# The gate product as seven block products, with its operands made during the MLP and kept in DRAM

## The chip, the core and the metric

The kernel runs on one core of one Trainium2 chip. The metric is device time in microseconds (us): the median over executions of the whole program. The core has a matrix engine (PE, with its weight loads shown apart as PEld), a vector engine (DVE), a scalar engine (ACT), a general engine (POOL), and a queue engine (SP) that issues nearly all of the DMAs. Each engine executes its own list of instructions in order; semaphores tie the lists together. Data lives in SBUF (128 partitions), PE writes to eight PSUM banks, and tensors too large for SBUF go to DRAM.

## The reference

One transformer layer over 1024 + 256 = 1280 tokens of width 1024: attention of two kinds, an output projection, a squared-ReLU MLP of inner width 4096, then the stage that the change rewrites, and a final norm. Its last part is

```python
n2 = _rms_norm(h, g_mlp, NORM_EPS)
a = jax.nn.relu(jnp.einsum('bsd,df->bsf', n2, w_ff1))
h = h + jnp.einsum('bsf,fd->bsd', a * a, w_ff2)

gate = jax.nn.sigmoid(jnp.einsum('bsd,de->bse', _rms_norm(h, g_ple, NORM_EPS), w_ple_gate))
h = h + gate * jnp.einsum('bsp,pd->bsd', p_l, w_ple_proj)
return h                      # then _rms_norm(h, g_final, NORM_EPS)
```

The gate product is 1280 x 1024 by 1024 x 1024; the embedding product is 1280 x 256 by 256 x 1024.

## The kernel before

Every matrix product is made of three: each fp32 operand is split into a high part (rounded to the format that PE reads fast, an ACT copy) and a low part (the rest, a subtraction on DVE or POOL), and high x high, high x low and low x high are summed in one PSUM bank. In the code this is `split3` (L156) or a list of pairs such as (a, b).

The MLP already uses a scheme of seven block products in place of eight (Strassen's, in Winograd's form). Tokens, inner width and columns are each halved; with HP = 5 token tiles of 128 in a half. Its second product, h += (a*a) w_ff2, is the loop over m = 0 to 55: seven block products in the order `O2 = (1, 7, 6, 4, 5, 3, 2)`, of eight steps m each. `put2(m)` is one step on PE: for each of the five tiles six matmuls of 512 columns, into five banks that are held over the eight steps. `prep(m)` makes the operands of step m: ACT writes the high parts of `ao` (128x1280) and `wo` (128x1024), and DVE the low parts. For products 7 and 5 DVE also subtracts two raw weight pieces (`w2r`, 128x1024), and for 7 and 6 POOL updates the kept piece `kt` (128x1024) for the next block product. `prep(m + 3)` is written behind `put2(m)`, since `ao` and `wo` have three slots each; so an operand set is made while PE is two steps ahead of its use. `load2(m)` fetches from DRAM two steps earlier still. After the last step of a block product, `evac2` adds the five banks into the quarters of h: product 6, the third, has the most of it, with fifteen adds on DVE and ten on POOL.

The gate stage takes the ten token tiles one after the other, FORD, each with both column halves: `gate_input` transposes the tile on PE (eight transposes), splits it, and computes the row scale; `gate(i)` runs 24 matmuls of 512 columns per half (the last tile's second half in two pieces of 256 columns), then the sigmoid: exp on ACT, a `tensor_scalar` on DVE, ln and exp on ACT, a multiplication on POOL (`gd`), and a `scalar_tensor_tensor` on DVE. `embed` is six matmuls per half; `add` multiplies (DVE, from PSUM), subtracts into h (POOL; DVE for the last two tiles) and sums squares (ACT). The final norm scales each half on DVE and stores it. The weights of the gate product (g_ple times w_gate, split) and of the embedding are made in SBUF towards the end of the MLP.

The order on each engine comes from a scheduler that simulates the program once at build time; the kernel's own code order is where it starts from. What it places is fixed at run time, and each engine waits at the head of its list.

Of the kernel before, what the change touches and what calls it, by code (L numbers as in the profile page):

```python
# [23 lines left out]
P = 128  # L24
# [21 lines left out]
def encoder_kernel(ctx: ExitStack, tc: tile.TileContext, x, xT, pT, w_in, w_out, w_ff1, w_ff2, w_gate, w_proj,  # L46
# [161 lines left out]
    def open_slots(pool_, tags):  # L208
        for tag in tags:
            slot_pool[tag] = pool_  # L210
            size = {"H": 2560, "L": 2560, "W": 1024, "Q": 1280, "K": 1280, "T": 512}[tag[0]]
            slot(tag, [P, size], F32, tag)
# [1128 lines left out]
    open_slots(fq, ["Q2", "Q3"])  # L1341
# [8 lines left out]
    AOS, WOS, ARS, WRS = ("H0", "H2", "H3"), ("H1", "L7", "L5"), ("L1", "L6"), ("W8", "W9", "Q0", "Q1", "Q2", "Q3")  # L1350
# [3 lines left out]
    kt2 = {}  # L1354
    wr_n = itertools.count()
    w2v = w_ff2.rearrange("(b c x r) n -> b x r c n", c=2, x=2, r=P)

    def load2(m):
# [3 lines left out]
        t = AR[m] = slot(ARS[m % 2], [P, 2, HT], F32, "ar")  # L1362
        dma(t, ad[i][b].rearrange("c p t -> p c t"))
        WR[m] = []
        for x, y in WSRC[i]:
            if i == 1:
                t = kt2[b] = slot(KTS[b], [P, 2, 512], F32, "kt2")
            else:
                t = slot(WRS[next(wr_n) % 6], [P, 2, 512], F32, "w2r")
                WR[m].append(t[:])  # L1370
            dma(t, w2v[b, x][:, :, y * 512:y * 512 + 512])
# [29 lines left out]
    def load_h(half, n, tag):  # L1401
# [4 lines left out]
    BANKS = ("f2 pj f1 f2 tr", "pj tr f1 f2 pj", "f2 tr f1 pj tr", "f2 pj f1 f2 tr", "tr pj f1 f2 pj",  # L1406
             "f1 f2 tr tr pj", "f1 f2 pj f1 f2")
# [68 lines left out]
    FORD = [TORD[2 * j + h] for h in (1, 0) for j in range(HP)]  # L1476
    gw, pw, n3 = [], [], {}
    g_n = itertools.count()

    def w_raw(src):  # L1480
        n = next(g_n)
        t = slot("W10" if n < 4 else f"W{8 + n % 2}", [P, D], F32, "graw")
        dma(t, src)
        return t

    def gate_w(k, tags):
        raw = w_raw(w_gate[k * P:(k + 1) * P, :])
        if len(tags) == 1:
            t = at32(tags[0], [P, 2, D], F32R, "gw")
            a, b = t[:, 0], t[:, 1]  # L1490
        else:
            a, b = (slot(t, [P, D], F32R, "gw")[:] for t in tags)
        S.activation(a, raw, AF.Copy, scale=gple[:, k:k + 1])
        V.scalar_tensor_tensor(b, raw, gple[:, k:k + 1], f(a), op0=ALU.mult, op1=ALU.subtract)
        gw.append((a, b))

    def proj_w(k, tag):
        raw = w_raw(w_proj[k * P:(k + 1) * P, :])
        t = at32(tag, [P, 2, D], F32R, "pw")
        S.activation(t[:, 0], raw, AF.Copy)  # L1500
        V.tensor_tensor(t[:, 1], raw, f(t[:, 0]), op=ALU.subtract)
        pw.append((t[:, 0], t[:, 1]))

    gi_n = itertools.count()

    def h_half(t, n):
        j, half = divmod(TORD.index(t), 2)
        return h_of(j, half, n)

    def gate_input(t):  # L1510

        n3_ = at32(("H5", "L4")[next(gi_n) % 2], [P, 2, KD, P], F32R, "n3")
        n3h, n3l = n3_[:, 0], n3_[:, 1]
        for n in range(2):
            tr = pp2[0].tile([P, 4, P], F32, tag="tr", name="trg", bufs=2)
            for k in range(4):
                PE.transpose(tr[:, k], h_half(t, n)[:, k * P:(k + 1) * P], ident)
            S.activation(n3h[:, 4 * n:4 * n + 4], tr, AF.Copy)
            V.tensor_tensor(n3l[:, 4 * n:4 * n + 4], tr, f(n3h[:, 4 * n:4 * n + 4]), op=ALU.subtract)
        ss = gq_.tile([P, 2], F32, tag="gss", name="gss")  # L1520
        for n in range(2):
            jk = gq_.tile([P, 512], F32, tag="gjk", name="gjk", bufs=1)
# [174 lines left out]
```

## Time and profile before

| what | value |
|---|---|
| time, median of 3 runs | 1690.53 us (1689.94 to 1693.5) |
| the profiled execution's own time | 1691.84 us |
| its span in the trace | 1690.1 us |
| PE busy over the span | 1651.6 us (98%) |
| DVE, ACT, POOL busy | 1179.9, 868.0, 661.0 us |
| second product of the MLP | about 1152 to 1535 us |
| gate stage | about 1535 us to the end |
| last matmul's end | about 1679 us |

Times in the trace are counted from the span's start. A row of the timeline gives the start, the duration, the engine, the line, the operation, output<-inputs, how many, and in brackets how long the engine was idle before and what ended that. A row of groups ends in busy time and the mean duration in ns. The view of one line gives min/median/max in ns. The table by windows gives each engine's busy time in a stretch, the granted PE clock (1.00 is full), the share of the DMA engines that was busy, and GB/s. PE's busy time is modelled, so it is read together with the distances between matmuls.

### The profile page before, as it was taken

Reading aid. Unit: us, or ns where it says so; the run is one execution under the profiler, and the core shown is the slowest. Engines: PE = TensorE matmul, PEld = TensorE weight load, DVE = VectorE, ACT = ScalarE, POOL = GpSimd, SP = SyncE. Lnnn points to the kernel's source line nnn. Section 1 sums busy time; section 2 is a strip of 40 time slices with the busy share of each in tenths; the row PEclk is TensorE's granted clock in tenths of the full one; section 3 lists DMA queues with packets and bytes.
Section 4 is the critical chain, followed back from the end, with each engine's and each line's share of the span. In section 5 each row is a group of like instructions: output and inputs, shape, how many; then the busy total and the mean of one; then the engine's idle time right before and its main releaser. Section 6 shows DMA issues by size and latency. Waiting matters only on the chain.

```text
span 1690.1 us, 27269 instructions
## 1 busy us (share of the span) xinstructions
PE 1651.6 (98%) x9849; PEld 1482.7 (88%) x9849; DVE 1179.9 (70%) x2119; ACT 868.0 (51%) x1749; POOL 661.0 (39%) x647
## 2 busy tenths in 40 slices
PE   8999999999899999999999999999999999999997
PEld 8999888888788888889999999998888888888886
DVE  7778588777888888668666666666665855445666
ACT  8643377776766667674333333233433333354554
POOL 1223455555654445433566665620532400001441
PEclk9999999999999999999999999999999999999999
DMA  9766843433954524395443343349676356532111
GB/s 309 239 216 237 247 144 110 133 108 98 273 161 130 154 74 131 108 330 172 160 136 131 132 159 128 135 169 386 220 225 203 124 192 210 177 117 75 35 44 50
DMA packets 191867, 278.28 MB, mean 165 GB/s; under 512 B 13674, under 2 KB 121076, under 8 KB 191732
## 3 DMA queue, kind: packets, MB, share of 16 engines
q1 hardware_dynamic: 189988, 271.28, 49.7%
q0 software_dynamic: 1600, 5.24, 1.0%
q8 instruction: 78, 1.28, 0.3%
q14 instruction: 57, 0.47, 0.1%
q10 hardware_dynamic: 144, 0.00, 0.0%
HBM read 182.63 MB, written 88.61 MB: 160 GB/s over the span
## 4 chain that ended last, share of the span: by engine, by line
PE 79%; DVE 8%; ACT 4%; issue 4%; POOL 2%; DMA 2%; POOLq 0%; SPq 0%; ACTq 0%; DVEq 0%
PE psa L264 6%; PE sc L651 6%; PE av L729 5%; PE psb L264 4%; PE pso L264 4%; PE tr L705 4%; PE psv L264 2%; PE psg L1588 1%; DVE pl L716 1%; DVE p L686 1%; DMA xt<-in_x 1%; POOL hq L1615 1%; DMA xr<-in_xT 1%; PE f__15605 L156 1%; PE f__16642 L156 1%
## 5 line engine op out<-in xcount | busy, mean ns | idle before, releaser
L1384 ACT ACTIVATE ao<-ar 128x1280 fp32r<-128x1280 f32 x56 | 71.2, 1273 | 183.7 <-PE f__15946 L156 36.6
L651 PE MATMUL sc<-kt,qt 128*128 128x512 f32 (+1 forms) x576 | 156.6, 392 | 8.8 <-ACT p L676 6.1
L716 DVE TENSOR_TENSOR pl<-tr,ph 128x512 fp32r<-128x512 f32 x204 | 138.0, 685 | 32.0 <-ACT ph L711 30.8
L1386 DVE TENSOR_TENSOR ao<-ar,ao 128x1280 fp32r<-128x1280 f32 x56 | 93.3, 1666 | 85.2 <-ACT ao L1384 85.2
L711 ACT ACTIVATE ph<-tr 128x512 fp32r<-128x512 f32 x204 | 120.0, 596 | 59.2 <-PE tr L705 52.7
L651 PEld LDWEIGHTS sc<-kt,qt 128*128 128x128 f32 x576 | 98.8, 189 | 27.1 <-ACT p L676 7.6
L264 PE MATMUL pso<-ow,mt 128*128 128x512 f32 x480 | 119.9, 396 | 2.0 <-DVE osq L756 1.3
L705 PE MATMUL tr<-ident,p 128*128 128x128 f32 x768 | 116.0, 274 | 5.8 <-DVE pl L716 5.1
L1588 PE MATMUL psg<-gw,n 128*128 128x512 f32 (+1 forms) x504 | 113.7, 381 | 0.0
L705 PEld LDWEIGHTS tr<-ident,p 128*128 128x128 f32 x768 | 91.6, 141 | 22.6 <-DVE pl L716 9.0
L1105 POOL TENSOR_SCALAR w1r<-w1r,gmlp 128x256 f32<-128x256 f32 x112 | 80.3, 735 | 68.4 <-DMA w1r<-in_w_ff 68.4
L1588 PEld LDWEIGHTS psg<-gw,n 128*128 128x128 f32 x504 | 90.9, 188 | 17.8
L264 PEld LDWEIGHTS pso<-ow,mt 128*128 128x128 f32 x480 | 88.0, 189 | 19.9 <-DVE osq L756 2.0
L729 PE MATMUL av<-ph,vt 128*128 128x256 f32 x544 | 101.8, 288 | 1.0 <-ACT ph L711 0.4
L690 POOL TENSOR_SCALAR p<-p,rl 128x1024 f32<-128x1024 f32 x64 | 76.2, 1192 | 50.6 <-DVE rl L688 49.1
L1178 ACT ACTIVATE w<-w1s 128x512 fp32r<-128x512 f32 x56 | 35.2, 629 | 114.7 <-POOL w1s L1185 55.3
L668 DVE TENSOR_REDUCE mm<-sc 128x1 f32<-128x1024 f32 (+1 forms) x80 | 84.2, 1056 | 9.4 <-PE sc L651 9.0
L729 PE MATMUL av<-pl,vt 128*128 128x256 f32 x408 | 89.4, 300 | 0.0
L729 PEld LDWEIGHTS av<-ph,vt 128*128 128x128 f32 x544 | 81.8, 188 | 6.4 <-DVE osq L756 0.8
L676 ACT ACTIVATE p<-sc,mm 128x1024 f32<-128x1024 f32 x64 | 71.4, 1116 | 25.1 <-DVE mm L668 16.3
L664 DVE CUSTOM_DVE_ANT_0 p<-sc,dist 128x1024 f32<-128x1024 f32 x64 | 77.6, 1218 | 7.8 <-PE sc L651 3.8
L673 ACT ACTIVATE p<-p,mm 128x1024 f32<-128x1024 f32 x64 | 73.5, 1149 | 18.0 <-DVE mm L664 17.2
(1520 smaller groups left out, 4705.9 us busy)
## 6 DMA issues: line engine op xcount, KB each, us to landing
ar<-ad SPq DMA_DIRECT2D x56, 640.0 KB, 4.0
w2r<-in_w_ff SPq DMA_DIRECT2D x56, 512.0 KB, 4.6
qt<-qd SPq DMA_DIRECT2D x160, 128.0 KB, 3.0
ad<-q SPq DMA_DIRECT2D x64, 320.0 KB, 2.8
ad<-qs SPq DMA_DIRECT2D x48, 320.0 KB, 2.2
w1r<-in_w_ff SPq DMA_DIRECT2D x28, 512.0 KB, 4.3
md<-ml SPq DMA_DIRECT2D x40, 256.0 KB, 2.5
mt<-md SPq DMA_DIRECT2D x20, 512.0 KB, 5.7
```

Of the source, the lines that this page charges most:

```text
L264: PE.matmul(ps, a, b, start=i == 0, stop=i == n - 1)
L651: PE.matmul(ps[:, h0:h0 + n], shared["q"][:, cc, v, i * P:(i + 1) * P], kt[:, s0 + h0:s0 + h0 + n], start=v == 0, stop=v == 1)
L664: V.tensor_tensor_reduce(out=p[:, :sn], in0=ps[:, :sn], in1=dst_t[:, off:off + sn], scale=SLOPES[idx], scalar=3.0e38, op0=ALU.add, op1=ALU ...
L668: V.tensor_reduce(out=st["m", i][:, 0:1], in_=ps[:, :sn], axis=AX.X, op=ALU.max, negate=True)
L690: G.tensor_scalar(p[:, :sn], p[:, :sn], rl[:, 0:1], 1.0, op0=ALU.mult, op1=ALU.mult)
L705: PE.transpose(t[:, jj, i * P:(i + 1) * P], st["ws"][i][:, j * P:(j + 1) * P], ident)
L711: S.activation(ph, st["tr", j2], AF.Copy)
L716: V.tensor_tensor(pl, st["tr", j2], f(st["ph", j2][:]), op=ALU.subtract)
L729: PE.matmul(st["av"][:, :256], x_, y_, start=j2 == 0 and n == 0, stop=j2 == nj - 1 and n == len(pr) - 1)
L1105: G.tensor_scalar(raw[:, k], raw[:, k], gmlp[:, 4 * kh + k:4 * kh + k + 1], 1.0, op0=ALU.mult, op1=ALU.mult)
L1386: V.tensor_tensor(ao[:, 1], a, f(ao[:, 0]), op=ALU.subtract)
L1588: ends[:] = [PE.matmul(ps, a, b, start=m == 0, stop=m == len(pr) - 1)]
```

## The change

The gate product is cut as the MLP's products are: tokens in two halves of five tiles, inner width and columns in halves of 512, and seven block products in place of eight, in the order `ORDER = (1, 2, 6, 5, 3, 7, 4)`. A block product is five tiles of twelve matmuls (four inner pieces of 128, times three). Products 1, 6 and 5 only feed sums (`m1`, `u3`); after each tile of products 2, 3, 7 and 4 one quarter of the gate is complete: `gate_half` adds the sum to the bank (DVE, from PSUM), takes the sigmoid, and combines. The tile's final norm follows after product 3 (second token half) and product 4 (first). After product 7 POOL multiplies the tile's h by `gfin` ahead, and for these halves ACT does the last scaling.

Operands of the token side are transposed quarters of h (`RA`): three of the four quarters are transposed during the last three block products of the MLP, the fourth in the gate stage; POOL and DVE form the sums and differences (four operations on 128x512 per tile), and `a_op` splits them. Operands of the weight side are made by `gate_operands`, a generator that the MLP's loop advances once per step from m = 4 on: for each half x of the pieces it loads four raw pieces, scales them by g_ple (POOL, 8 x 128x512), forms differences (POOL, 4 x 128x1024), and splits each of seven operands in two pieces (`out`: ACT copy, DVE subtraction, store of 512 KB to `bed`). The embedding's weights (4 x 512 KB) and embeddings (10 x 256 KB) go the same way to `pwd` and `ped`. The gate stage loads them back (`b_ops`, `proj_w`, `embed_in`). PSUM banks "tr" are freed of the MLP's fifth and sixth block product; slots in SBUF are shared out anew.

```diff
@@ the MLP's loop
     for m in range(NM):
         put2(m)
         if m in QUADS:
             load_h(*QUADS[m])
         if m + 3 < NM:
             prep(m + 3)
-        if m >= 4 * NB and m % 4 == 0 and len(gw) < 4:
-            gate_w(len(gw), KTS[2 * len(gw):2 * len(gw) + 2])
...
+        n, b = divmod(m, NB)
+        if m >= 4:
+            with tc.issue_after(fetched[0].ins):
+                next(made, None)
+        if n == 4 and b < HP:
+            if b == 0:
+                raw_tokens("H5", 12)
+            S.activation(RA[12][:, b], quad_tr(12, b), AF.Copy)
...
@@ gate_operands
+        def out(y, src, dst):
+            S.activation(stage[:, y, 0], src, AF.Copy)
+            V.tensor_tensor(stage[:, y, 1], src, f(stage[:, y, 0]), op=ALU.subtract)
+            dma(dst, f(stage[:, y]))
+
+        for x in range(2):
...
+            for t, k0, c0 in ((r11, 4, 0), (r22, 0, 512), (r12, 4, 512), (r21, 0, 0)):
+                k0 += 2 * x
+                dma(t, w_gate[k0 * P:(k0 + 2) * P, c0:c0 + 512].rearrange("(k p) c -> p k c", p=P))
+                for y in range(2):
+                    G.tensor_scalar(t[:, y], t[:, y], gple[:, k0 + y:k0 + y + 1], 1.0, op0=ALU.mult, op1=ALU.mult)
+            yield
+            for i, t, a, b, op in ((1, r11, None, None, None), (3, r22, None, None, None), (2, r21, None, None, None),
+                                   (7, r22, r22, r12, ALU.subtract), (5, r12, r12, r11, ALU.subtract),
+                                   (6, r11, r11, r22, ALU.add), (4, r21, r21, r11, ALU.subtract)):
+                if op is not None:
+                    G.tensor_tensor(t, a, b, op=op)
+                for y in range(2):
+                    out(y, t[:, y], bed[i][2 * x + y])
+                yield
@@ gate stage
-            for k in range(KD):
-                pr += [(n3h[:, k], gw[k][0][:, n]), (n3h[:, k], gw[k][1][:, n]), (n3l[:, k], gw[k][0][:, n])]
...
+    def product(i, j, c0=0, cn=512):
+        ps = bank(next(gslots), "psg")[:, :cn]
+        pr = []
+        for k in range(4):
+            a, w = AOPS[i][j], BOPS[i][k]
+            c = slice(c0, c0 + cn)
+            pr += [(a[:, 0, k], w[:, 0, c]), (a[:, 0, k], w[:, 1, c]), (a[:, 1, k], w[:, 0, c])]
...
+        ps, _ = product(i, j)
+        e = e_tile()
+        V.tensor_tensor(e, ps, acc_, op=ALU.add)
+        if i == 7:
+            V.tensor_tensor(m1[:, j], ps, m1[:, j], op=ALU.add)
+        sigmoid(e, e, rn, late)
+        combine(half, j, 512 * n, 512, e, embed(p, 512 * n, 512), n, late)
+        if i in (3, 4):
+            finish(half, j)
+        elif i == 7:
+            h = h_of(j, half, 1)
+            G.tensor_tensor(h, h, gfin[:, 1], op=ALU.mult)
```

What this does to the order of instructions is seen at three places. In all of them `ao`, `wo`, `w2r` and `kt` belong to the MLP's second product, as above.

The first is DVE's list around the MLP's second to third block product (products 7 and 6), before:

```order
L1379 TENSOR_TENSOR w2r<-w2r 128x1024
L1387 TENSOR_TENSOR wo<-w2r,wo 128x1024
L1386 TENSOR_TENSOR ao<-ar,ao 128x1280
L1387 TENSOR_TENSOR wo<-w2r,wo 128x1024
L1386 TENSOR_TENSOR ao<-ar,ao 128x1280
L1387 TENSOR_TENSOR wo<-w2r,wo 128x1024
L1386 TENSOR_TENSOR ao<-ar,ao 128x1280
L1387 TENSOR_TENSOR wo<-kt_14319,wo 128x1024
```

and in the change (`gbs` is the stage from which the gate's weight operands are stored, `gr` the raw pieces):

```order
L1384 TENSOR_TENSOR w2r<-w2r 128x1024
L1392 TENSOR_TENSOR wo<-w2r,wo 128x1024
L1391 TENSOR_TENSOR ao<-ar,ao 128x1280 x2
L1534 TENSOR_TENSOR gbs<-gr,gbs 128x512
L1392 TENSOR_TENSOR wo<-w2r,wo 128x1024
L1534 TENSOR_TENSOR gbs<-gr,gbs 128x512
L1391 TENSOR_TENSOR ao<-ar,ao 128x1280
L1392 TENSOR_TENSOR wo<-kt_14320,wo 128x1024
L1391 TENSOR_TENSOR ao<-ar,ao 128x1280
L1534 TENSOR_TENSOR gbs<-gr,gbs 128x512 x2
```

The subtractions of the gate's weights stand between those of the MLP's operands, which PE waits for; in DVE's list there are 23 of them from just ahead of the first `wo` of product 7 to just behind the first `wo` of product 4.

The second is POOL's list in the same stretch. Before, it holds only the updates of `kt` and the adds into h:

```order
L1390 TENSOR_TENSOR kt_14497<-w2r,kt_14497 128x1024
L1428 TENSOR_TENSOR hq<-hq,acc 128x512 x5
L1390 TENSOR_TENSOR kt_14548<-w2r,kt_14548 128x1024
L1390 TENSOR_TENSOR kt_14594<-w2r,kt_14594 128x1024
L1390 TENSOR_TENSOR kt_14634<-w2r,kt_14634 128x1024
L1390 TENSOR_TENSOR kt_14676<-w2r,kt_14676 128x1024
```

In the change:

```order
L1545 TENSOR_SCALAR gr<-gr,gple 128x512 x8
L1395 TENSOR_TENSOR kt_14389<-w2r,kt_14389 128x1024
L1433 TENSOR_TENSOR hq<-hq,acc 128x512 x3
L1551 TENSOR_TENSOR gr<-gr 128x1024
L1433 TENSOR_TENSOR hq<-hq,acc 128x512 x2
L1395 TENSOR_TENSOR kt_14495<-w2r,kt_14495 128x1024
L1551 TENSOR_TENSOR gr<-gr 128x1024
L1395 TENSOR_TENSOR kt_14545<-w2r,kt_14545 128x1024
L1551 TENSOR_TENSOR gr<-gr 128x1024
L1395 TENSOR_TENSOR kt_14635<-w2r,kt_14635 128x1024
L1551 TENSOR_TENSOR gr<-gr 128x1024
```

Scalings and differences of the gate's weights (`gr`) stand among the updates of `kt`; a second set of both follows in product 6.

The third is POOL's list in the gate stage. Before, one tile half takes two operations, and a tile a third (`p_l`):

```order
L1569 TENSOR_TENSOR p_l<-pr,p_h 128x256
L1596 TENSOR_TENSOR gd<-gd,ge 128x512
L1615 TENSOR_TENSOR hq<-hq,ge 128x512
L1596 TENSOR_TENSOR gd<-gd,ge 128x512
L1615 TENSOR_TENSOR hq<-hq,ge 128x512
```

In the change, around product 7 of the gate (L1756 is the multiplication ahead by `gfin`; a tile that lies in the `gfin` slot carries its name):

```order
L1658 TENSOR_TENSOR gd<-gd,ge 128x512
L1756 TENSOR_TENSOR hq<-hq,gfin 128x512 x2
L1666 TENSOR_TENSOR hq<-hq,ge 128x512
L1658 TENSOR_TENSOR gd<-gd,gfin 128x512
L1658 TENSOR_TENSOR gd<-gd,ge 128x512
L1756 TENSOR_TENSOR hq<-hq,gfin 128x512
L1666 TENSOR_TENSOR hq<-hq,gfin 128x512
```

A tile half there takes three operations. On PE the list has 432 matmuls of the gate product where it had 504 (24 of them of 256 columns, before 48), and 80 transposes of h in both.

More of the change, by code (lines that the diff above doesn't have):

```diff
@@ new lines, in encoder_kernel, with e_tile @@
+    e_n = itertools.count()
+    gfin = None
+    def e_tile():
+        if gfin is not None:
+            n = next(e_n) % 7
+            if n % 2:
+                return gfin[:, 2 + n // 2]
+        return gq_.tile([P, 512], F32, tag="ge", name="ge", bufs=4)[:]
+    def product(i, j, c0=0, cn=512):
+        ps = bank(next(gslots), "psg")[:, :cn]
+        pr = []
+        for k in range(4):
+            a, w = AOPS[i][j], BOPS[i][k]
+            c = slice(c0, c0 + cn)
+            pr += [(a[:, 0, k], w[:, 0, c]), (a[:, 0, k], w[:, 1, c]), (a[:, 1, k], w[:, 0, c])]
+        ends = []
+        for n, (a, w) in enumerate(pr):
+            ends[:] = [PE.matmul(ps, a, w, start=n == 0, stop=n == len(pr) - 1)]
+        return ps, ends[0]
```

379 lines of the change are left out of this document (235 added, 144 removed).

## The prediction

> **What bounds the kernel now.** I read the busy times first, then the table by windows, since an average over stages says little.
>
> ```profile
> PE 1651.6 (98%) x9849; PEld 1482.7 (88%) x9849; DVE 1179.9 (70%) x2119; ACT 868.0 (51%) x1749; POOL 661.0 (39%) x647
> ...
> 1200.00:1250.00 50.00, 50.00 (x222) 41.42 (x221) 37.95 (x20) 20.47 (x21) 25.29 (x10) 1.00 0.71 228
> ...
> 1625.00:1650.00 25.00, 25.00 (x116) 20.75 (x115) 14.48 (x25) 13.70 (x38) 10.85 (x9) 1.00 0.08 27
> ...
> 1675.00:1691.00 16.00, 4.08 (x29) 3.62 (x27) 9.53 (x25) 6.68 (x19) 0.00 (x0) 0.74 0.18 66
> ```
>
> The second column is PE. In the MLP's second product and in the gate stage it never rests, at full clock; it stops about 1679, some 11 us before the end. So a matmul removed from either stage is worth its whole slot, as long as nobody else becomes late. The 1650 us of PE elsewhere are untouched: up to the MLP's second product the lists of the two programs agree.
>
> **The matmuls removed.** The timeline of PE and the groups of the gate product give the slot.
>
> ```profile
> 1333.02 1.52 PE L156 MATMUL f__15608<-wo,ao 128*128 128x512 f32 x6
> 1334.38 1.52 PE L156 MATMUL f__15609<-wo,ao 128*128 128x512 f32 x6
> ...
> L1588 PE MATMUL psg<-gw,n 128*128 128x512 f32 x456 | 107.9, 392 | 0.0
> ...
> L1588 PE MATMUL psg<-gw,n 128*128 128x256 f32 x48 | 5.9, 283 | 0.0
> ```
>
> Six matmuls start every 1.36 us, so one costs 0.227 us (the mean of 392 ns overlaps its neighbours); one of 256 columns costs 5.9 / 48 = 0.123. The gate has 456 + 48 of them in the trace and will have 408 + 24: 48 x 0.227 + 24 x 0.123 = **13.8 us less**. Embedding matmuls and transposes keep their numbers. A step m of the MLP lasts 5 x 1.36 = 6.80 us.
>
> **What the change adds, and where it lies.** By size it is work for DVE and POOL, both only part busy. But the two do not run freely side by side:
>
> ```profile
> 1230.10 1.22 DVE L1387 TENSOR_TENSOR wo<-w2r,wo 128x1024 fp32r<-128x1024 f32 x1
> 1230.32 3.25 POOL L1390 TENSOR_TENSOR kt<-w2r,kt 128x1024 f32<-128x1024 f32 x1 [3.88 <-issue]
> 1231.24 3.69 DVE L1386 TENSOR_TENSOR ao<-ar,ao 128x1280 fp32r<-128x1280 f32 x1
> ...
> 1597.85 1.31 POOL L1596 TENSOR_TENSOR gd<-gd,ge 128x512 f32<-128x512 f32 x1 [2.71 <-issue]
> 1598.24 0.69 DVE L1519 TENSOR_TENSOR n<-trg,n 128x512 fp32r<-128x512 f32 x1 [1.02 <-ACT n L1518]
> ```
>
> POOL's `kt` needs 2.4 us alone (below); started 1 us before DVE's `wo` ended, it took 3.25. The `ao` behind it needs 1.5 alone and took 3.69: it ended 1.36 after POOL did. So a DVE operation with two SBUF operands and a POOL operation go one after the other. A DVE operation that reads PSUM (`trg`) took its usual 0.69 beside POOL. I therefore add DVE's two-operand work and POOL's into one queue. Durations alone, as min/median/max of a line, and the distance of neighbours:
>
> ```profile
> 1315.52 0.68 DVE L1428 TENSOR_TENSOR acc<-acc,f__15262 128x512 f32<-128x512 f32 x1
> 1316.11 0.68 DVE L1428 TENSOR_TENSOR hq<-hq,acc 128x512 f32<-128x512 f32 x1
> ...
> L1386 DVE TENSOR_TENSOR ao<-ar,ao x56: 1478/1493/3694, 1139.2 to 1514.7; 128x1280 fp32r<-128x1280 f32 x56
> L1387 DVE TENSOR_TENSOR wo<-w2r,wo x32: 1211/1218/3423, 1194.2 to 1516.1; 128x1024 fp32r<-128x1024 f32 x32
> L1379 DVE TENSOR_TENSOR w2r<-w2r x16: 1217/1226/3409, 1130.3 to 1399.2; 128x1024 f32<-128x1024 f32 x16
> L1392 POOL TENSOR_TENSOR kt<-w2r,kt x8: 2388/2400/2406, 1251.6 to 1299.1; 128x1024 f32<-128x1024 f32 x8
> L1428 POOL TENSOR_TENSOR hq<-hq,acc x15: 1274/1823/2533, 1204.9 to 1331.9; 128x512 f32<-128x512 f32 x15
> L1105 POOL TENSOR_SCALAR w1r<-w1r,gmlp x112: 474/482/1708, 779.6 to 1085.8; 128x256 f32<-128x256 f32 x112
> ```
>
> Neighbours on DVE start 0.08 us closer than they last, so I count 1.40 for `ao`, 1.13 for `wo`, 1.14 for `w2r`, 0.60 for 128x512; on POOL 2.39, 1.29, and for a scaling of 128x512, twice the size of the one shown, between 0.48 and 0.96: 0.70.
>
> **The MLP's second product.** Take the 17 operand sets of m = 8 to 24, which PE gives 17 x 6.80 = 115.6 us. Now: 17 x (1.40 + 1.13) + 10 x 1.14 on DVE, 15 x 2.39 + 5 x 1.29 on POOL: 54.4 + 42.3 = 96.7, or 84%. The order puts into the same stretch 23 `gbs` (13.8), six to eight differences of 2.39 (14.3 to 19.1), and 16 scalings (11.2): 39 to 44 more, 136 to 141 in all. The excess is 20 to 25 us; as some of the first scalings can go in ahead, I take 20. The copies of ACT (two of about 0.6 a step, ACT being busy 20 of 50 us) fit.
>
> How much of it may PE not notice?
>
> ```profile
> 1301.91 1.27 ACT L1384 ACTIVATE ao<-ar 128x1280 fp32r<-128x1280 f32 x1 [4.58 <-PE f__15264 L156]
> 1304.63 1.22 DVE L1387 TENSOR_TENSOR wo<-kt,wo 128x1024 fp32r<-128x1024 f32 x1
> ...
> 1315.31 1.52 PE L156 MATMUL f__15605<-wo,ao 128*128 128x512 f32 x6
> ...
> 1326.56 2.31 DVE L1387 TENSOR_TENSOR wo<-kt,wo 128x1024 fp32r<-128x1024 f32 x1
> 1328.91 1.55 PE L156 MATMUL f__15605<-wo,ao 128*128 128x512 f32 x6
> ```
>
> An operand set is begun when PE frees its slot (ACT waited 4.58 us for that), is ready at 1305.85, and PE uses it at 1315.31: 9.5 us in hand. Two sets later, behind the many adds after the third block product, it is ready at 1328.87 for a use at 1328.91. So that reserve exists, and is already spent once, at this very place. What arrives there late comes on top, and PE stalls by it: **20 us**, between 0 (nothing of POOL's new work is needed in time) and 25. The generator's steps stand between the operand sets in all three lists, so no set can overtake them.
>
> **The gate stage.** Its rows:
>
> ```profile
> L1615 POOL TENSOR_TENSOR hq<-hq,ge 128x512 f32<-128x512 f32 x16 | 22.4, 1400 | 36.3 <-DVE ge L1613 36.3
> L1596 POOL TENSOR_TENSOR gd<-gd,ge 128x512 f32<-128x512 f32 x16 | 20.7, 1293 | 64.0 <-ACT ge L1595 36.7 <-issue 14.8 <-ACT rf L140 8.3
> L1644 DVE SCALAR_TENSOR_TENSOR hq<-hq,rf,gfin 128x512 f32<-128x512 f32 x19 | 13.5, 748 | 0.3
> L1597 DVE SCALAR_TENSOR_TENSOR ge<-gd,ge 128x512 f32<-128x512 f32 x19 | 13.1, 689 | 6.0 <-POOL gd L1596 5.9
> L1593 DVE TENSOR_SCALAR gd<-ge 128x512 f32<-128x512 f32 x19 | 8.2, 432 | 7.3 <-ACT ge L1592 7.3
> L144 DVE SCALAR_TENSOR_TENSOR rf<-rfv,rfu 128x1 f32<-128x1 f32 x10 | 1.6, 160 | 0.9
> ```
>
> PE's time per tile of a completing product falls from 24 + 6 matmuls a half (6.8 us) to 12 + 6 (4.08). Products 1, 2, 6 and 5 leave room: POOL's 20 operand sums (26 us) and their gates are caught up within 6 and 5, where PE needs 13.6 us each and little else happens. The last three products have none. Per tile, in the common queue: product 3 POOL 2 x 1.29, DVE 0.60 + 0.35 (the `tensor_scalar`) + 2 x 0.70 (final norm) + 0.4 (three one-column operations) + 0.36 (three splits in five tiles) = 5.7; product 7 POOL 3 x 1.29, DVE 0.95 = 4.8; product 4 2.58 + 0.95 + 0.70 + 0.4 = 4.6. Up to the fourth tile of product 4: 28.5 + 24 + 18.4 = 71 against 14 x 4.08 = 57 on PE. Of the excess of 14 some 4 lie in today's tail too (the last pieces' exp waits for ACT and DVE there), so I take **10 us**, between 0 and 14. Adds from the products' banks read PSUM and are left out. The loads from `bed` (22 MB in a stage whose DMA share is 0.08) are hidden.
>
> **The sum**, against the profiled execution's own 1691.84: 1691.84 - 13.8 + 20 + 10 = 1708; the median of the runs is 1.3 lower: **1707 us**.
>
> **Rivals.** *All hidden.* The generator's results are needed only in the gate stage; if the excess before the third block product ends stays at nothing, PE keeps its 1.36 us and the gain stands: 1690.5 - 13.8 = 1677, or 1687 with the gate stage's 10. For it: DVE is idle 12 of 50 us in the window shown, ACT for more than half. Against it: the sum of the two, 63 of 50 (waits for each other included), and the reserve spent at 1328.9. It decides where the excess drops below about 1 us. 15% for 1677, 13% for 1687.
>
> *Only the MLP.* Gates of different tiles overlap so well that the last three products keep pace: 1697. 10%.
>
> *The DMA queue.* By the shapes, the generator stores 28 + 4 pieces of 0.52 MB and 10 of 0.26, and loads 6.5 MB: 26 MB in 28 steps of 6.8 us, 136 GB/s more.
>
> ```profile
> 1140.00:1150.00 10.00, 10.00 (x71) 10.00 (x70) 9.57 (x15) 4.04 (x4) 2.41 (x1) 1.00 1.04 400
> ar<-ad SPq DMA_DIRECT2D x2, 640.0 KB, 11.9
> ...
> w2r<-in_w_ff SPq DMA_DIRECT2D x6, 512.0 KB, 4.4
> ```
>
> At 400 GB/s a load lands after 11.9 us (those issued from 1140 to 1160), at 242 after 4.4 (1220 to 1240). A stage half is written again only when its store has landed, one step later: copy, subtraction and 4.4 us make about 6, in 6.8. At 12 us two such steps in a row would be 15 late: 1722.
>
> *The clock.* A PE that has rested starts slowly.
>
> ```profile
> 5.75 0.41 PE L156 MATMUL psb<-wlp,xh 128*128 128x256 f32 x1
> 5.97 0.41 PE L156 MATMUL psb<-whp,xl 128*128 128x256 f32 x1
> ...
> 15.00:18.00 3.00, 3.00 (x28) 3.00 (x27) 0.51 (x2) 2.58 (x8) 0.00 (x0) 1.00 0.86 297
> ...
> 1682.00:1684.00 2.00, 0.00 (x0) 0.00 (x0) 1.79 (x8) 1.47 (x6) 0.00 (x0) 0.67 0.00 0
> ```
>
> At the program's start matmuls of 256 columns come 0.22 us apart, for some 4 us, and later 28 in 3 us; after PE's last one at 1679.1 the granted clock is down by 1682 to 1684. So a rest of 3 to 5 us costs about 2 us more. Five such rests in the MLP would make 10: 1717. Against it: a set is late by a few us at most, and PE then has 6.8 us of work again. [...] DMA and clock together 12%, at 1717 to 1722.
>
> **Chances.** 50% for 1707 (own range 1697 to 1714), 15% 1677, 13% 1687, 10% 1697, 12% above 1714. The range leaves out the fully hidden case and little at the top: 1682 to 1721. A measurement of this kernel tells 0.2%, 3.4 us, from no change: faster 22% (1677, half of 1687), same 8%, slower 70%.
>
> **What would show it.** In the profile after, PE has idle time in the second and third block products with DVE's `ao` or `wo` as releaser, `gbs` and `ao` show means far above 0.6 and 1.5 us, and POOL's `gr` differences far above 2.4; in the last 60 us of the gate stage PE waits and the stretch from its last matmul to the end grows. Wrong would be: PE rows 1.36 us apart through the MLP, or stalls that end on a DMA.

## The result, and the profile after

The changed kernel took 1717.6 us (median of four runs, 1715.5 to 1719.0), the kernel before 1692.0 us beside it. The ratio is 1.015, 95% interval 1.0131 to 1.0169: slower. The forecast was 1707. The profiled execution of the changed kernel took 1718.2 us with a span of 1716.4, 26.3 us more than the 1690.1 of before.

It lies above the likeliest case's own range (1697 to 1714) and inside the whole one (1682 to 1721). The first two fences are the page's busy line of the changed kernel and the table by windows (columns: length, PE, PE's weight loads, DVE, ACT, POOL, granted clock, DMA share, GB/s).

```profile
PE 1647.7 (96%) x9777; PEld 1472.5 (86%) x9777; DVE 1253.1 (73%) x2159; ACT 897.5 (52%) x1774; POOL 757.4 (44%) x695
```

```profile
1200.00:1250.00 50.00, 42.83 (x183) 35.01 (x182) 46.90 (x24) 20.62 (x24) 41.18 (x15) 0.93 0.75 253
1230.00:1240.00 10.00, 2.83 (x9) 1.97 (x8) 10.00 (x4) 2.10 (x3) 8.84 (x3) 0.72 0.58 175
...
1300.00:1350.00 50.00, 44.95 (x189) 36.39 (x188) 48.84 (x33) 17.90 (x21) 38.00 (x17) 0.94 0.68 235
...
1646.00:1670.00 24.00, 22.73 (x98) 17.86 (x97) 23.95 (x42) 14.19 (x35) 13.43 (x10) 1.00 0.48 161
1650.00:1700.00 50.00, 40.42 (x178) 31.52 (x177) 48.17 (x72) 27.96 (x63) 35.16 (x25) 0.97 0.32 107
```

PE has holes in three places: twice in the MLP's second product (7 and 5 us) and in the last third of the gate stage. In all three DVE is busy for 47 to 49 of 50 us and POOL for 35 to 41. The row from 1646 to 1670 shows the start of the last one: DVE is full there, while POOL works 13 of 24 us. The waits that PE had (engine, tile and line, what ended the wait: us in all, times, longest), and one of ACT's:

```profile
PE f__14979 L156 <- DVE ao L1391: 7.2, 1, 7.2
PE f__15780 L156 <- DVE wo L1392: 4.6, 1, 4.6
PE f__16120 L156 <- DVE hq L1451: 1.5, 1, 1.5
...
PE psp L156 <- DVE ge L1664: 6.8, 4, 2.4
PE psp L156 <- DVE gfin L1664: 6.0, 3, 3.6
...
ACT gbs L1533 <- DMA bed<-gbs: 49.1, 13, 10.6
```

The MLP's waits end on operand splits (`ao`, `wo`), those of the gate on the multiplication by the sigmoid that frees an embedding's PSUM bank (L1664). ACT waits 49 us for stores to land, a second suspect. What DVE and POOL did before the wait of 7.2 us, from the timeline:

```profile
1219.64 3.64 POOL L1395 TENSOR_TENSOR kt<-w2r,kt 128x1024 f32<-128x1024 f32 x1
...
1220.95 3.41 DVE L1392 TENSOR_TENSOR wo<-w2r,wo 128x1024 fp32r<-128x1024 f32 x1
...
1223.24 3.38 POOL L1551 TENSOR_TENSOR gr<-gr 128x1024 f32<-128x1024 f32 x1
1224.29 5.69 DVE L1534 TENSOR_TENSOR gbs<-gr,gbs 128x512 fp32r<-128x512 f32 x2
1226.59 2.84 POOL L1395 TENSOR_TENSOR kt<-w2r,kt 128x1024 f32<-128x1024 f32 x1
...
1234.34 7.21 DVE L1391 TENSOR_TENSOR ao<-ar,ao 128x1280 fp32r<-128x1280 f32 x2
```

In the rows shown, `wo` and the second `gbs` end 1.1 and 0.6 us after the POOL operation beside them, and the stretched operations last two to four times as long as before: `wo` lasts 3.41 instead of 1.2, two `gbs` 5.69 instead of 1.3, two `ao` 7.21 instead of 2.9. Behind them PE stands, and starts slowly again:

```profile
1238.03 2.08 PE L156 MATMUL f__14979<-wo,ao 128*128 128x512 f32 x4 [7.17 <-DVE ao L1391]
1239.90 1.72 PE L156 MATMUL f__14980<-wo,ao 128*128 128x512 f32 x4
1241.45 1.08 PE L156 MATMUL f__14981<-wo,ao 128*128 128x512 f32 x4
...
1683.35 1.66 PE L156 MATMUL psp<-pw,p_hl 128*128 128x512 f32 x6 [3.63 <-DVE gfin L1664]
...
1695.38 2.93 PE L156 MATMUL psp<-pw,p_hl 128*128 128x512 f32 x6 [2.17 <-DVE ge L1664]
```

In the gate stage, groups of DVE by form (busy, mean ns of one):

```profile
L1717 DVE SCALAR_TENSOR_TENSOR hq<-hq,rf,gfin 128x512 f32<-128x512 f32 x14 | 14.2, 1042 | 0.2
...
L1664 DVE TENSOR_TENSOR ge<-psp,ge 128x512 f32<-128x512 f32 x13 | 8.9, 682 | 0.2
...
L1655 DVE TENSOR_SCALAR gd<-ge 128x512 f32<-128x512 f32 x13 | 8.6, 665 | 1.8 <-ACT ge L1654 1.8
...
L144 DVE SCALAR_TENSOR_TENSOR rf<-rfv,rfu 128x1 f32<-128x1 f32 x10 | 6.9, 695 | 0.4
```

The operations that read PSUM (L1664) keep their 0.68 us (0.69 before). The final norm goes from 0.748 to 1.042, the `tensor_scalar` from 0.432 to 0.665, a one-column operation (L144) from 0.16 to 0.70.

**Where the 26.3 us are.** The second MLP product starts 2.2 us later (1154.28 for 1152.09). From there to the gate's first matmul it takes 406.7 us instead of 382.9, 23.8 more. In that lie 44 of the 80 transposes, which stood in the gate stage before; five groups of four lengthen a block product by 2.4 us (54.4 to 56.8), so 5.2 of the 23.8 are a move, and **18.6 are loss**. The gate stage, from its first matmul to the end, takes 155.4 instead of 155.1. With 13.8 us of matmuls and 5.2 of transposes gone it should take 136.1: **19.3 are loss**. 2.2 + 18.6 - 13.8 + 19.3 = 26.3. The 2.2 us are not shown to be the change's: the changed kernels of the experiments, whose code is the same up to there, start this product between 1149.6 and 1154.9.

Of the 18.6, PE's waits are 13.7. Of the 19.3, its waits are 12.8, 1.0 is a longer tail behind the last matmul (12.0 us for 11.0), and 5.5 are matmuls that ran slower or further apart between the waits.

### The profile page after: what moved, and what is told of

Same layout as the page of the kernel before. It is cut to its first block, busy times and chain, and to the rows that moved or that the text cites. A ratio compares the mean times of both kernels' runs of the same rounds, so it can differ in the third digit from the quotient of the medians.

```text
span 1716.4 us, 27453 instructions
## 1 busy us (share of the span) xinstructions
PE 1647.7 (96%) x9777; PEld 1472.5 (86%) x9777; DVE 1253.1 (73%) x2159; ACT 897.5 (52%) x1774; POOL 757.4 (44%) x695
## 3 DMA queue, kind: packets, MB, share of 16 engines
q8 instruction: 77, 1.26, 0.3%
## 4 chain that ended last, share of the span: by engine, by line
PE 71%; DVE 12%; DMA 6%; issue 5%; ACT 3%; POOL 3%; SPq 1%; ACTq 0%; DVEq 0%; POOLq 0%
PE psa L264 6%; PE sc L651 6%; PE av L729 5%; PE pso L264 4%; PE tr L705 4%; PE psb L264 3%; PE psg L1688 2%; PE psv L264 2%; DVE ao L1391 1%; DMA w2r<-in_w_ff 1%; DMA xt<-in_x 1%; DVE hq L1717 1%; DVE gbs L1534 1%; DVE pl L716 1%; DMA xr<-in_xT 1%
## 5 line engine op out<-in xcount | busy, mean ns | idle before, releaser
L1391 DVE TENSOR_TENSOR ao<-ar,ao 128x1280 fp32r<-128x1280 f32 x56 | 104.5, 1869 | 76.3 <-ACT ao L1389 76.3
L1389 ACT ACTIVATE ao<-ar 128x1280 fp32r<-128x1280 f32 x56 | 71.0, 1269 | 103.6 <-PE f__16489 L156 26.3
L1688 PE MATMUL psg<-gbo,gao 128*128 128x512 f32 (+1 forms) x387 | 92.3, 385 | 0.0
L1688 PEld LDWEIGHTS psg<-gbo,gao 128*128 128x128 f32 x387 | 71.0, 188 | 15.0
L673 ACT ACTIVATE p<-p,mm 128x1024 f32<-128x1024 f32 x64 | 73.5, 1149 | 17.9 <-DVE mm L664 17.2
```

Of the source, the lines that this page charges most:

```text
L1391: V.tensor_tensor(ao[:, 1], a, f(ao[:, 0]), op=ALU.subtract)
L1688: ends[:] = [PE.matmul(ps, a, w, start=n == 0, stop=n == len(pr) - 1)]
```

## The experiments

The theory was the prediction's: DVE operations with two SBUF operands and POOL operations go one after the other, and this common queue is overfull at both places. The rivals: the stores of the generator (ACT is held, the DMA queue is full), DVE's own sum of work, and, in the gate stage, too few PSUM banks. The expectations put the two losses at 19 us in the MLP and 18.6 in the gate stage, where the account above has 18.6 and 19.3. All ratios are to the kernel before, run on the same chip.

### The stores left out (`e2_no_store`)

Left out are 24 of the 28 stores of the gate's weight blocks.

```
-    bed = {i: [dp.tile([P, 2, 512], F32, name=f"bed{i}_{k}") for k in range(4)] for i in range(1, 8)}
+    bed = {i: [dp.tile([P, 2, 512], F32, name=f"bed{i}_{k}") for k in range(4)] for i in (1,)}
...
-            dma(dst, f(stage[:, y]))
+            if dst is not None:
+                dma(dst, f(stage[:, y]))
...
-                    out(y, t[:, y], bed[i][2 * x + y])
+                    out(y, t[:, y], bed[1][2 * x + y] if i == 1 else None)
...
-            dma(f(t[:]), bed[i][k])
+            dma(f(t[:]), bed[1][k])
```

> Leaves out 24 of the 28 stores of the generator's weight blocks (only block product 1's are stored, and every block product of the gate takes its weights from those four), so the output is not the reference's; every copy, scaling, difference and subtraction stays. Common queue of DVE and POOL: it is not the stores that make PE wait; ACT's 49 us of waits for the landing of stores go, but DVE and POOL keep their work, so PE's 19 us of stalls in the MLP's second product stay to within 4 us and the time is 1713 to 1720. Stores (ACT held until a store lands, saturated DMA): the 19 us go, about 1699.

Measured: 1727.6 us, ratio 1.0209 (1.0191 to 1.0227). Neither number came out, but the verdict on the stores is plain: without them the kernel is 10 us slower still. PE's waits in the MLP grow from 13.7 to 18.2 us, 17.2 of them on the same operand splits. The windows of the splits `gbs` on DVE (busy, count) in the changed kernel

```profile
1200.00:1250.00 50.00, 10.75 (x6) 0.93 0.75 253
1250.00:1300.00 50.00, 11.03 (x10) 1.00 0.96 340
```

and without the stores

```profile
1200.00:1250.00 50.00, 20.96 (x10) 0.90 0.59 192
1250.00:1300.00 50.00, 24.55 (x14) 0.97 0.59 199
```

show 24 splits instead of 16 in the same 100 us, and twice their time. The landing of the stores had spread the generator's work; without it more falls into the crowd. That the stores held it back is read from these counts and from ACT's 49 us, not tried by itself.

### The generator on DVE (`e3_gen_on_dve`)

```
-                    G.tensor_scalar(t[:, y], t[:, y], gple[:, k0 + y:k0 + y + 1], 1.0, op0=ALU.mult, op1=ALU.mult)
+                    V.tensor_scalar(t[:, y], t[:, y], gple[:, k0 + y:k0 + y + 1], 1.0, op0=ALU.mult, op1=ALU.mult)
...
-                    G.tensor_tensor(t, a, b, op=op)
+                    V.tensor_tensor(t, a, b, op=op)
...
-            G.tensor_tensor(hl[:, 1, :, :cn], raw, f(hl[:, 0, :, :cn]), op=ALU.subtract)
+            V.tensor_tensor(hl[:, 1, :, :cn], raw, f(hl[:, 0, :, :cn]), op=ALU.subtract)
```

> The generator's 16 scalings, 8 differences and 3 splits of POOL go to DVE; same output. Common queue: a difference of 128x1024 holds the queue 1.14 us instead of 2.39, a scaling 0.35 instead of 0.70; seven differences and 16 scalings in the crowded stretch save 9 + 6 = 14 us, so of 19 us of PE stalls about 5 are left: about 1704 (1700 to 1709), although DVE gets more to do. DVE and POOL side by side, each bounded by its own sum: DVE was busy 47 of 50 us there and gets 14 us more, so PE waits longer: 1722 to 1732. Stores: no change, 1717.

Measured: 1708.6 us, ratio 1.0101 (1.0079 to 1.0123). The common queue's range held; DVE got more to do and the kernel became 9 us faster. PE's waits in the MLP are 7.2 us instead of 13.7.

```profile
1200.00:1250.00 50.00, 46.62 (x198) 37.75 (x197) 47.27 (x30) 20.44 (x26) 26.55 (x10) 0.97 0.81 264
```

DVE is as busy as with POOL's help (47.3 for 46.9 us), but makes 30 operations instead of 24 in that time: what it no longer spends on waiting pays for the added work. POOL's busy time fell from 41.2 to 26.6.

### The generator late (`e4_gen_late`), and late on DVE (`e5_late_dve`)

```
-        if m >= 4:
+        if m >= 24:
             with tc.issue_after(fetched[0].ins):
                 next(made, None)
+                if m % 3 == 0:
+                    next(made, None)
```

> The generator starts at operand set 24 instead of 4 and makes two steps at every third set; same work, same output. Common queue: from set 24 on POOL has no work of the MLP and DVE only 2.5 to 3.7 us a set, so both kinds of work fit in 6.8 us a set; the MLP's 19 us of PE stalls go to 0 to 4: 1699 to 1703. Stores: two steps at a set need two landings of 5 to 6 us on ACT inside 6.8 us, so ACT falls behind and PE stalls in the later block products instead: 1710 or more.

> The late generator, and its scalings, differences and splits on DVE instead of POOL; same output. Common queue: the late generator left 6.2 us of PE stalls in the MLP, all in the stretch 1350 to 1400 where POOL worked 18.6 us; with DVE's shorter holds (a difference 1.14 for 2.39, a scaling 0.35 for 0.70) they go to 0 to 2: 1698 to 1701. DVE by its own sum: it was busy 41.5 of 50 us there and gets 9 more: no gain over the late generator, 1703 or slower.

Measured: 1703.4 us (1.0072, 1.005 to 1.0094), and 1702.4 (1.0056, 1.0039 to 1.0073). The first is 0.4 us above the queue's range, the second 1.4: right in kind, with a rest. The gate starts at 1550.6 and 1546.0 instead of 1560.95. The profiled run of the first took 1708.0 us, the slowest of its four. The two times are not clearly apart (the intervals overlap), and 1702.4 lies between what the queue (1698 to 1701) and DVE's own sum (1703 or slower) gave for the second, so by its time that run decides nothing. The longest wait that is left is a new one, at the boundary between two block products. DVE and PE of the late generator:

```profile
1376.94 1.23 DVE L1384 TENSOR_TENSOR w2r<-w2r 128x1024 f32<-128x1024 f32 x1 [3.15 <-DMA w2r<-in_w_ff]
1378.09 0.68 DVE L1451 TENSOR_TENSOR hq<-f__15623,hq 128x512 f32<-128x512 f32 x1
...
1378.83 2.01 PE L156 MATMUL f__16043<-wo,ao 128*128 128x512 f32 x6 [2.66 <-DVE hq L1451]
```

DVE waits 3.15 us for a weight load, and the add that frees a PSUM bank stands behind it. Here the prediction's rival of the DMA queue is real, though small: the window from 1350 to 1400 has a DMA share of 0.88, and 0.94 with the generator on DVE, where the stalls left in the MLP go from 6.2 to 4.0 us and not to 0 to 2.

### More banks for the embedding (`g2_banks`)

```
-    gslots = itertools.cycle(("f2", "pj", "f1"))
+    gslots = itertools.cycle(("f2", "f1"))
+    eslots = itertools.cycle(("tr", "pj"))
...
-        pq = bank("tr", "psp")[:, :cn]
+        pq = bank(next(eslots), "psp")[:, :cn]
```

> In the gate stage the products use four PSUM banks instead of six and the embedding four instead of two; nothing else changes. Common queue: DVE and POOL have more work for the last three products than PE, so PE's 12.8 us of waits for embedding banks go, but the end is set by DVE and POOL and stays: 1713 to 1718. Latency with two banks: the chain from a product to the multiplication that frees its embedding bank is longer than two tiles of 4.08 us, and with four banks it need not be shorter; the 12.8 us and the slow clock behind them go: 1700 to 1705.

Measured: 1719.3 us (1.016, 1.0143 to 1.0177): no gain, 1.3 us above the queue's range and far from the other. PE's waits for embedding banks that end on DVE fall from 12.8 to 2.8 us, and the end stays where it was.

```profile
PE psp L156 <- DMA p_hl<-ped: 4.2, 1, 4.2
...
PE psp L156 <- DVE ge L1665: 1.4, 1, 1.4
...
PE psp L156 <- DVE gd L1656: 1.2, 1, 1.2
```

So the releaser named in PE's waits was a symptom. Given more banks, PE runs ahead and the end is set by the engines behind it. The new wait for a load, 4.2 us, follows from them too: SP issues that load of `p_hl` at 1677.2, directly behind two stores of the output that stand ahead of it in SP's list, and SP waits for the final norm on DVE before such stores (40 us in all from 1640 on).

### POOL's work in the gate stage given to DVE (`g3_sig_dve`, `g5_gate_dve`)

```
-        (V if late else G).tensor_tensor(d, d, e, op=ALU.mult)
+        V.tensor_tensor(d, d, e, op=ALU.mult)
```

and in `g5` beside it

```
-        (V if late else G).tensor_tensor(h, h, e, op=ALU.subtract)
+        V.tensor_tensor(h, h, e, op=ALU.subtract)
...
-            G.tensor_tensor(h, h, gfin[:, 1], op=ALU.mult)
+            V.tensor_tensor(h, h, gfin[:, 1], op=ALU.mult)
```

> In the gate stage the sigmoid's first product goes from POOL to DVE in all tiles; same output. Common queue: 0.69 us less a tile (0.60 for 1.29), 14 tiles in the last three products: 71 us become 61 against PE's 57; DVE's own sum with its reads of PSUM becomes 4.9, 3.7 and 3.9 us a tile, 58 us. The gate's loss falls from 18.6 to about 9: 1706 to 1710. DVE by its own sum alone (busy 47 of 50 us from 1650 to 1700) gets 8 us more: 1722 to 1727.

> All of POOL's work on the gate's tiles (the sigmoid's product, the residual's subtraction, the product with the final gain) goes to DVE; same output. Common queue alone: 31 operations by 0.69 are 21 us less, the gate's loss goes: about 1699. Larger of two bounds (the queue, and DVE's own sum with its reads of PSUM, which the prediction left out): DVE then has 5.5, 4.9 and 4.5 us a tile, 70 us for PE's 57, as much as the queue had: no better than the sigmoid's product alone, 1710 to 1718.

Measured: 1715.8 us (1.0138, 1.0123 to 1.0153) and 1712.2 (1.0117, 1.0102 to 1.0132). The first misses both its ranges, the second is inside that of the two bounds. From the gate's first matmul to the end the two take 155.4 and 149.8 us; the changed kernel 155.4. The window of 1650 to 1700 with the sigmoid's product on DVE

```profile
1650.00:1700.00 50.00, 39.63 (x169) 31.24 (x167) 49.89 (x81) 28.17 (x65) 22.06 (x16) 0.90 0.29 93
```

and with all of it on DVE

```profile
1650.00:1700.00 50.00, 41.04 (x180) 32.86 (x178) 49.12 (x109) 30.80 (x73) 0.00 (x0) 0.92 0.34 109
```

has DVE without a pause. With POOL silent the final norm is back at 749 ns, the `tensor_scalar` at 434 and L144 at 157, and DVE is still full: 109 operations instead of 72. Then it is its own sum that counts, with the reads of PSUM in it, which last the same with POOL busy and silent (L1664 682 and 691 ns, L1747 682 and 689) but take 0.6 us each: the expectation's 70 us for PE's 57 are 13 too many, and the stage's loss is 149.8 - 136.1 = 13.7.

In the first of the two runs another wait may hide part of what its edit gained: 6.3 of PE's 10.7 us of waits in the gate stage end on loads of `p_hl`, where the changed kernel has none.

```profile
1688.25 2.90 PE L156 MATMUL psp<-pw,p_hl 128*128 128x512 f32 x6 [4.43 <-DMA p_hl<-ped]
```

SP issued this load at 1685.26, again directly behind two output stores that waited for a final norm on DVE. The loads issued ahead of the stores were not tried, so that moving the sigmoid's product gained nothing is not shown to be DVE's sum alone.

### The final gain in PSUM (`g6_gain_psum`)

```
-    gslots = itertools.cycle(("f2", "pj", "f1"))
+    gslots = itertools.cycle(("f2", "f1"))
...
-            V.scalar_tensor_tensor(h, h, rf, gfin[:, n], op0=ALU.mult, op1=ALU.mult)
+            V.scalar_tensor_tensor(h, h, rf, gps[n], op0=ALU.mult, op1=ALU.mult)
...
+            gps = [pj("gps"), pj("gps")]
+            for n in range(2):
+                S.activation(gps[n], gfin[:, n], AF.Copy)
```

> From product 3 on the final gain lies in two PSUM banks (the products keep four of six), so that the final norm's DVE operations have one operand in PSUM; same operations, same output. Common queue: those operations leave it, two a tile in product 3 and one in product 4, 14 x 0.70 = 10 us of 71; DVE's own sum of 52 us does not change. The gate's loss falls by 5 to 10: 1707 to 1713. If what counts is how long DVE is busy with its own work and not whom it waits for: 1716 to 1720, as with the banks alone.

Measured: 1713.2 us (1.0124, 1.0109 to 1.014), 4.5 us less, at the upper edge of the queue's range; the gate stage takes 150.8 us. This is the cleanest test of the mechanism: the same operation, on the same engine, with one operand in another memory.

```profile
L1659 DVE SCALAR_TENSOR_TENSOR ge<-gd,ge 128x512 f32<-128x512 f32 x13 | 14.0, 1076 | 1.2 <-POOL gd L1658 1.2
L1717 DVE SCALAR_TENSOR_TENSOR hq<-hq,rf,gps 128x512 f32<-128x512 f32 x14 | 10.0, 740 | 0.2
```

The final norm's mean falls from 1042 to 740 ns, about its duration with POOL silent (749 in `g5`); the operation in the line above, whose operands stayed in SBUF, keeps its 1076. The number of SBUF operands does not tell it alone, though: the `tensor_scalar` (L1655), which has one, took 765 ns in this run and 665 in the changed kernel, against 434 with POOL silent. Why that one is stretched no run shows.

### The sigmoid's refinement left out (`g4_no_refine`)

```
-        (V if late else G).tensor_tensor(d, d, e, op=ALU.mult)
-        V.scalar_tensor_tensor(e, d, -2.0, e, op0=ALU.add, op1=ALU.mult)
```

> Leaves out the sigmoid's refinement in the gate stage (POOL's product and DVE's operation behind it), so the gate has the wrong sign and the output is not the reference's. Common queue: 14 x (1.29 + 0.60) = 26 us less in the last three products; the gate's loss of 18.6 goes, PE waits for no embedding bank: 1696 to 1702. If something else set the end there (loads, ACT's chain of exp and logarithm): above 1710.

Measured: 1701.9 us (1.0056, 1.0041 to 1.0071). The gate stage takes 141.0 us instead of 155.4, and PE's waits for embedding banks fall to 1.4 us. Work taken from both engines, rather than moved between them, wins back most of the gate's loss: 14.4 of the 19.3 us.

```profile
1650.00:1700.00 50.00, 33.90 (x164) 28.07 (x162) 33.88 (x74) 30.79 (x78) 18.78 (x15) 0.86 0.35 117
```

### The best of the change, and its control (`c2_gain_psum`, `c1_plain_sigmoid`, `b_plain_sigmoid`)

Both versions of the change have the generator on DVE, placed thus:

```
-        stage = slot("L6", [P, 2, 2, 512], F32R, "gbs")
+        stage = slot("L4", [P, 2, 2, 512], F32R, "gbs")
...
+    STEPS = (24, 25, 26, 27, 29, 31, 33, *range(35, 46))
-        if m >= 4:
+        if m in STEPS:
             with tc.issue_after(fetched[0].ins):
                 next(made, None)
+                if m < 27:
+                    next(made, None)
```

`c2` adds the gain in PSUM. `c1` and the control, which is the kernel before, have the plain sigmoid:

```
-        (V if late else G).tensor_tensor(d, d, e, op=ALU.mult)
-        V.scalar_tensor_tensor(e, d, -2.0, e, op0=ALU.add, op1=ALU.mult)
...
-        (V if late else G).tensor_tensor(h, h, e, op=ALU.subtract)
+        (V if late else G).tensor_tensor(h, h, e, op=ALU.add)
```

> The same placing of the generator, the refinement kept, and the final gain in PSUM; same output as the reference's. Common queue: 1702.4 less 2 in the MLP and less 5 to 10 in the gate: 1690 to 1696, about level with the kernel before. DVE by its own sum: 1700 to 1702.

> The generator on DVE, made in sets 24 to 45 with gaps where the loads are heavy (stage in another slot, free until set 48), and the sigmoid without its refinement, as exp(-ln(1+x)) gives it, the residual added instead of subtracted. Sum: 1702.4 with the late generator on DVE, 15.7 less as the gate without the refinement showed, 2 less if the gaps remove half of the 4 us of PE stalls left in the MLP: 1685 (1682 to 1689), faster than before. If the two gains share one wait, or the late steps stall PE behind the loads: 1690 or more.

> The kernel before (gate as four accumulated products), with the sigmoid without its refinement as in the fastest version of the change: what that edit is worth without the block products. PE never waits in its gate stage, so only the tail behind the last matmul (11 us, DVE and ACT) can get shorter, by the POOL and DVE operations on its way: 0 to 2 us, 1689 to 1692. If the refinement alone explained that version's 1688, this kernel would come out at 1688 or less.

| kernel | median, us | ratio to before | gate's first matmul to end, us |
|---|---|---|---|
| before | 1692.0 | 1 | 155.1 |
| changed | 1717.6 | 1.015 (1.0131 to 1.0169) | 155.4 |
| `c2`: generator late, on DVE; gain in PSUM | 1699.9 | 1.0044 (1.0032 to 1.0057) | 151.0 |
| `c1`: generator late, on DVE; plain sigmoid | 1688.0 | 0.9975 (0.9967 to 0.9984) | 140.0 |
| control: before with the plain sigmoid | 1687.6 | 0.9973 (0.9964 to 0.9982) | 152.4 |

`c2` missed the queue's range by 4 us and came out at the lower edge of the other, DVE by its own sum (1700 to 1702): the gain in PSUM was worth 3.5 us in the gate (154.5 with the late generator on DVE, 151.0 here), less than the 5 to 10 expected, and the MLP kept its stalls. `c1`, inside its range, is faster than both kernels, by 0.25% against before. But the control, which has no block products at all, is as fast. My expectation for it was 1689 to 1692, on the ground that PE never waits there; it went to the value that I had named as the sign that the refinement alone explains `c1`. The last matmul and the end of the two profiled executions tell where the block products' gain went. `c1`:

```profile
1674.01 0.97 PE L156 MATMUL psp<-pw,p_hl 128*128 128x256 f32 x6 [1.20 <-DVE ge L1665]
```

The control:

```profile
1677.23 0.28 PE L156 MATMUL psp<-pw,p_l 128*128 128x256 f32 x1
```

`c1` reaches its gate 13.3 us later than the control (1546.69 for 1533.39): 3.3 us are there when the second MLP product starts (before and the control, alike up to there, are themselves 1.6 apart, and the changed kernels up to 5.3), 5.2 are the moved transposes, and 4.8 are stalls, 3.9 of them two waits at the same block boundary as in the late generator. Its PE then needs 128.3 us in the gate instead of 144.1, where 13.8 and 5.2 less would be 125.1, and is done 2.5 us earlier; but its tail behind the last matmul is 11.7 us (to a span of 1686.7) against 8.3 (to 1685.8), since DVE and ACT still have the last tiles to finish. So 13.8 us of matmuls are saved, and 3.3 + 4.8 + 3.2 + 3.4 = 14.7 lost in four places, none of them large, the first of them not shown to be the change's. In the control the refinement's operations lay on the tail: 11.0 us in before, 8.3 without them. These 2.7 us are all that this pair of traces places of the control's 5.3 (1687.6 for 1692.9 beside it); another 1.6 are its earlier start.

## Why the prediction was right or wrong

- **The matmuls removed, 13.8 us:** right. PE makes 72 fewer (9849 to 9777), at an unchanged pace between the waits (six in 1.36 us), and its busy time falls even though it now has slow stretches.
- **The common queue:** right as a mechanism, shown by the gain in PSUM (1042 to 740 ns) and by the generator on DVE (faster with more work on the busier engine). As a bound on the time it was not enough: the sigmoid's product on DVE, the gain in PSUM with the generator late (`c2`) and the banks came out above its ranges. "A DVE operation that reads PSUM took its usual 0.69 beside POOL" held too: 0.68.
- **The MLP, 20 us:** 18.6 measured, 13.7 of it waits. Most of it belongs to the generator's place and engine: from the start of the second MLP product to the gate's first matmul the changed kernel takes 406.7 us, with the generator late 397.9, late and on DVE 393.1, so that 8.8 and 13.6 of the 18.6 go. The releasers are the forecast's, `ao` and `wo`; the waits lie in the second block product, as named, and in the fourth, behind the adds of the third, not in the third itself. The marks came out too: the splits `gbs` have a mean of 1.26 us (40.23 for 32), POOL's differences one of 3.2 (25.24 for 8).
- **The gate stage, 10 us, between 0 and 14:** wrong; 19.3 measured, above the upper bound, and this is the term that put the time above the likeliest case's own range. Its parts are above: waits of 12.8, a tail 1.0 longer, and 5.5 of slower or looser matmuls. Three steps failed:
  - The 4 us that were taken off for the tail did not lie there (next item).
  - The sum had nothing for what PE loses after a wait (the item on the clock).
  - "Adds from the products' banks read PSUM and are left out." They were not stretched (L1747: 682 ns, and 689 with POOL silent), but they hold DVE. With the multiplications that read the embedding's banks they are two a tile in products 3 and 4 and three in product 7, 14 tiles: 33 x 0.6 = 20 us. DVE's own work in the last three products is then about 50 us for PE's 57, before any waiting. Its waits for POOL come on top, some 32 us in the whole gate stage by the means against the times alone: 26 splits `gao` by 0.32, 13 refinements by 0.39, 14 norms by 0.29, ten L144 by 0.54, ten L143 by 0.38 and the rest.

  The bound that this suggests is DVE's own work plus what it waits for, not the queue alone. Two things speak for it: the row from 1646 to 1670 (DVE full, POOL at 13 of 24 us), and the gate stage with all of POOL's work on DVE (13 us too many, 13.7 lost). It would explain why moving one POOL operation to DVE gave nothing, all of them 5.6 us, and taking both operations away 14.4. No run takes the adds alone off DVE, so their share of the 19.3 us is argued, not shown.
- **"Some 4 us lie in today's tail too":** wrong. The tail behind the last matmul hardly grew (12.0 us for 11.0), and the excess was added ahead of it. The sign that the prediction named, a longer stretch behind the last matmul, is this 1.0 us.
- **All hidden (1677 or 1687), only the MLP (1697):** wrong for this placing. With the generator late and on DVE the MLP still loses 5.0 us, and the time is 1702, since the gate's loss stays (18.4).
- **The DMA queue:** ACT did wait 49 us for landings, as this rival says, and yet the stores are not what costs: without 24 of them the kernel is slower. The rival shows itself only where the queue is relieved, through a weight load 3 us late.
- **The clock:** the time came out at this rival's 1717, partly by its cause. The sum took nothing for it. After the wait of 7.17 us eight matmuls took 3.4 us from start to start where they take 1.8, at a granted clock of 0.50 from 1238 to 1240; after the one of 4.61 us eleven took 4.75 where they take 2.5, at 0.50 as well (1346 to 1350). Near the end six lost 1.4 us (0.56 from 1695 to 1697) and the last six of 256 columns 0.8 (0.50 from 1702.8 to 1704.4). That is some 6 us in four slow stretches, where the rival had five of 2 us. The price, about 2 us for a rest, fits; but the granted clock reads 1.00 through the slow matmuls at the program's start (5 to 10 us, 0.22 us apart), so of the two ends of the trace only the last shows the clock itself.
- **The sum:** against the forecast's 1708 for the profiled run, 1718.2 is 1.4 us less in the MLP, 9.3 more in the gate stage, and 2.2 of a later start. That the MLP's term came out so close is in part luck: it was reckoned as waiting alone, and 4.9 of the 18.6 us are not waits.

## What to carry to other kernels

Where DVE and POOL are both used, add up for each stage DVE's operations with two SBUF operands and POOL's as one queue (the final norm took 1042 ns here, and 749 with POOL silent), and DVE's whole work, with its PSUM reads and its waits, as a second bound; here a POOL operation cost DVE up to most of its own duration (one L144 took 1.27 us for 0.16 beside one of 1.44). The second bound is argued from this case, not proven. An operand kept in PSUM took the final norm out of that queue (740 ns), at the price of two PSUM banks and two copies. Before a faster version is credited to a change, give the same side edit to the kernel before: here the control took the whole gain.

## What was not expected

- One-column operations with two operands are stretched most for their size: L144's mean went from 160 to 695 ns, and is 157 with POOL silent (`g5`); one took 1.27 us beside a POOL operation of 1.44, and ended with it. It is not new, though: L143, which stands ahead of it, had a mean of 913 ns before and 596 after.
- PE slowed after shorter rests than expected. In the late generator six matmuls took 2.01 us after a wait of 2.66, the next twelve, behind another wait of 1.12, 2.93 and 2.51 where six take 1.52, and the granted clock is 0.93 over the window from 1350 to 1400; in the changed kernel six took 2.93 after 2.17 (0.56 from 1695 to 1697), at the end, where several rests follow each other. After 1.85 us (late generator on DVE) they took 1.66 (1.00 from 1350 to 1400), and after 3.63 in the changed kernel 1.66 too (the row is above; 1.00 from 1683 to 1685), so the length of one rest alone doesn't decide it. By the prediction's estimate, 3 to 5 us, the first two waits would have been harmless and the last one not; the measurement decides.
- A transfer's latency can help, as far as counts tell: ACT's waits for the stores spread the generator's operations (16 splits `gbs` from 1200 to 1300, 24 without 24 of the stores), and without them the kernel lost another 10 us.
